# Score products on 64 rows of the array, queries and keys without a copy

## The chip, the cores and the metric

The kernel runs on one core of one Trainium2 chip. A core has a matrix engine (TensorE, PE in the profile), two elementwise engines that matter here (VectorE or DVE, and ScalarE or ACT), GpSimd (POOL), and a queue (SyncE or SP) that issues the DMA transfers. The metric is the device time of one execution in microseconds. The time of the kernel before is 1354.46 us, the median of 3 runs (1352.4 to 1356.58).

## The reference, cut to what matters

Two layers of a diffusion block over 512 latent tokens and 256 context tokens, model width 1024, all in float32. The change concerns the mixer of the first layer, differential attention: 8 heads, and per head two softmax maps of head width 64 that share one value matrix of width 128.

```python
def project(t):
    q, k, v = jnp.split(t @ wqkv, 3, axis=-1)
    return (q.reshape(B, n, DA_HEADS, 2, HEAD_DIM),
            k.reshape(B, n, DA_HEADS, 2, HEAD_DIM),
            v.reshape(B, n, DA_HEADS, DA_VDIM))

def attend(qb, kk, vv):
    s = jnp.einsum('bqhmd,bkhmd->bhmqk', qb, kk) * scale
    p = jax.nn.softmax(s, axis=-1)
    p = p[:, :, 0] - lam_full * p[:, :, 1]
    return jnp.einsum('bhqk,bkhe->bqhe', p, vv)

q, k, v = project(h)                     # 512 latent tokens
q, k = apply_rope_2d(q, cos, sin), apply_rope_2d(k, cos, sin)
qc, kc, vc = project(hc)                 # 256 context tokens
k_all = jnp.concatenate([kc, k], axis=1)
```

After the mixer come its output projection, a SwiGLU feed-forward, a second layer with a gated short convolution and its own feed-forward, and a final norm.

## The kernel before, in words

**Precision.** TensorE reads 32-bit operands in a rounded form (`F32R`). To keep float32 accuracy, each operand is split into a high part (the rounded value) and a low part (the remainder): `split` (lines 54 to 56) rounds on ScalarE and subtracts on VectorE. A product is then hi*hi + hi*lo + lo*hi, three matmuls into one accumulator (`mm3`, lines 77 to 81).

**Layout.** Activations lie transposed: channels on the 128 partitions, tokens along the free dimension. One head's query projection is a tile of 128 partitions by 512 tokens; its first 64 partitions belong to map 0, the other 64 to map 1.

**Queries and keys of a head.** `proj_qk_steps` (line 468) loads and splits the weights, runs the projections (accumulators psq, psk and, for context keys, pskc) and calls `finish_q` and `finish_k`. Both rotate with `rope` (four VectorE instructions) and split into high and low part, in the staging tiles qt (128 x 2 x 512) and kt (128 x 2 x 768), of which there is one buffer each. Then `halves_to` (line 414) copies by DMA, on the SP queue, into one pair of tiles per map: for queries, the map's 64 rows are put twice, into the lower and the upper 64 partitions of qs0 or qs1; for keys, the high part goes to the lower 64 partitions of ks0 or ks1 and the low part to the upper 64. That is four transfers of 256 KB for queries and four of 192 KB for keys per head. With these tiles one matmul over 128 rows computes q_hi*(k_hi + k_lo), a second q_lo*(k_hi + k_lo).

**Scores.** `attend` (line 490) goes through four blocks of 128 queries per head. For each map it runs four matmuls at line 507 (two parts j by two column ranges, 512 and 256 keys) into a score tile S of 128 x 768 in PSUM, takes the row maximum on VectorE (line 511) and the exponential on ScalarE (line 515). There are two S buffers. Then the maps are combined (line 523), transposed on TensorE (pt, line 528), copied, and multiplied by the values (po, line 535).

**What sets the order.** The code runs under a tile scheduler, which decides the order of each engine's instructions at build time. Between one head's score products it places the projections of the next head (psq, psk, pskc), the value projection of the next pair of heads (psv), the modulation sums (ada, pada) and, in the last heads, the output projection (poa). Each engine then runs its list strictly in that order.

Of the kernel before, what the change touches and what calls it, by code (L numbers as in the profile page):

```python
# [11 lines left out]
F32 = mybir.dt.float32  # L12
F32R = mybir.dt.float32r
AF = mybir.ActivationFunctionType
ALU = mybir.AluOpType
# [3 lines left out]
P = 128  # L19
# [6 lines left out]
def block_kernel(  # L26
# [11 lines left out]
    nc = tc.nc  # L38
    T = x.shape[1]
# [4 lines left out]
    KV = T + C  # L44
    KB = KV // P
    NH = D // P
    HD = 64
# [6 lines left out]
    def split(hi, lo, src):  # L54
        nc.scalar.copy(hi, src)  # L55
        nc.vector.tensor_tensor(lo, src, hi.bitcast(F32), op=ALU.subtract)  # L56
# [55 lines left out]
    psB = tc.alloc_tile_pool(name="psB", bufs=2, space=PSUM)  # L112
# [8 lines left out]

    for tag, n, bufs in (
        [(f"Or{h}", 512, 1) for h in range(NH)] + [("qs0", 1024, 2), ("qs1", 1024, 2)]
        + [("e", 768, 3), ("pth", 768, 3), ("ptl", 768, 3), ("ks0", 768, 2), ("ks1", 768, 2)]
        + [(f"v{p}{t}", 256, 2) for t in range(KB) for p in "hl"]
        + [("sq", 512, 1), ("dg1", 512, 1)]
        + [(t, 4, 2) for t in ("sv", "sr", "rh", "rl")] + [(t, 4, 3) for t in ("rr", "mx")] + [("ss", 8, 2), ("den", 8, 2)]
        + [("ld", 2, 1)]
        + [("araw", 1024, 2), ("ada", 1024, 1), ("qt", 1024, 1), ("kt", 1536, 1), ("rcos", 512, 1), ("rsin", 512, 1)]
        + [("sw", 512, 1), ("rt", 512, 2)]  # L130
    ):
        ap.tile([P, n], F32, tag=tag, bufs=bufs, name=f"place_{tag}")
# [4 lines left out]
    xt_dram = nc.dram_tensor("xt_spill", [DB, P, T], F32, kind="Internal").ap()  # L137

    rows = lambda v: v.rearrange("(j p) -> j p", p=P)
    st1, st2 = (ap.tile([P, P], F32, tag=t, name=n) for t, n in (("ks1", "st1"), ("ks1", "st2")))  # L140
    nc.vector.memset(st1, 0.0)
    nc.vector.memset(st2, 0.0)
    nc.sync.dma_start(st1[0:8, :], rows(c[0]))
# [26 lines left out]
    cn = [nat(ctx, t, "qs1", 2, f"cn{t}") for t in range(CB)]  # L170
# [28 lines left out]
    def nat_rstd(src, tag, name):  # L199

        nb = len(src)
        ss = ap.tile([P, 8], F32, tag="ss", name=f"ss{name}")
        for t in range(nb):
            for f in range(2):
                junk = ap.tile([P, 512], F32, tag="sq", bufs=1, name=f"junk{name}")
                nc.scalar.activation(
                    junk, src[t][:, f * 512:(f + 1) * 512], AF.Square,
                    accum_out=ss[:, t + 4 * f:t + 4 * f + 1],
                )
        v = ap.tile([P, 4], F32, tag="sv", name=f"sv{name}")[:, :nb]  # L210
        nc.vector.tensor_tensor(v, ss[:, :nb], ss[:, 4:4 + nb], op=ALU.add)
        nc.vector.tensor_scalar(v, v, 1.0 / D, EPS, op0=ALU.mult, op1=ALU.add)
        r = ap.tile([P, 4], F32, tag="sr", name=f"sr{name}")[:, :nb]
        nc.gpsimd.tensor_tensor(r, v, mhalf[:, :nb], op=ALU.pow)
        ps = spread(r, nb, "pt", name)
        o = ap.tile([P, 512], F32, tag=tag, bufs=2 if tag == "ks0" else 1, name=f"rs{name}")[:, :nb * P]
        nc.vector.tensor_copy(o, ps)
        return o

# [40 lines left out]
    for k in range(0, DB, 2):  # L260
        pt = psB.tile([P, 2, T], F32, tag="S", name=f"ptx{k}")
        for a in range(2):
# [2 lines left out]
            nc.vector.tensor_copy(XT0[k + a], pt[:, a, :])  # L265
        if k == 0:
            ada0(0, raws0)
    rc = nat_rstd(cn, "ks0", "c")
    ctt = [ap.tile([P, 4, C], F32, tag="araw", name=f"ct{i}") for i in range(2)]
    CT = [ctt[k // 4][:, k % 4, :] for k in range(DB)]  # L270
    for i in range(2):
        pt = psB.tile([P, 4, C], F32, tag="S", name=f"ptc{i}")
        for a in range(4):
            k = 4 * i + a
# [126 lines left out]
    On = [None] * NH  # L401
    later = []

    def rope(ps, tmp, name):

        r = ap.tile([P, T], F32, tag="rt", name=f"rt{name}")
        b = ap.tile([P, T], F32, tag="sw", bufs=1, name=f"sw{name}")
        nc.vector.tensor_tensor(b, ps, rsin, op=ALU.mult)
        nc.vector.tensor_tensor(r, ps, rcos, op=ALU.mult)
        nc.vector.stream_shuffle(tmp, b, SWAP)  # L410
        nc.vector.tensor_tensor(r, r, tmp, op=ALU.add)
        return r

    def halves_to(dst, src, both):

        for m in range(2):
            s = src[64 * m:64 * m + 64]
            for d in range(2):
                o = dst[m][64 * d:64 * d + 64]
                nc.sync.dma_start(o.bitcast(F32), s if both else s[:, d, :])  # L420

    def finish_q(h, ps):

        qt = ap.tile([P, 2, T], F32, tag="qt", bufs=1, name=f"qt{h}")
        r = rope(ps, qt[:, 1, :], f"q{h}")
        nc.scalar.activation(qt[:, 0, :].bitcast(F32R), r, AF.Copy, scale=HD ** -0.5)
        nc.vector.scalar_tensor_tensor(
            qt[:, 1, :].bitcast(F32R), r, HD ** -0.5, qt[:, 0, :], op0=ALU.mult, op1=ALU.subtract
        )
        q = [ap.tile([P, 2, T], F32R, tag=f"qs{m}", name=f"qs{h}_{m}") for m in range(2)]  # L430
        halves_to(q, qt, True)
        return q

    def finish_k(h, ps, psc):

        kt = ap.tile([P, 2, KV], F32, tag="kt", bufs=1, name=f"kt{h}")
        r = rope(ps, kt[:, 1, :T], f"k{h}")
        split(kt[:, 0, T:].bitcast(F32R), kt[:, 1, T:].bitcast(F32R), psc)
        split(kt[:, 0, :T].bitcast(F32R), kt[:, 1, :T].bitcast(F32R), r)
        ks = [ap.tile([P, KV], F32R, tag=f"ks{m}", name=f"ks{h}_{m}") for m in range(2)]  # L440
        halves_to(ks, kt, False)
        return ks

    def finish_v(g, t, ps):
# [45 lines left out]
    def attend(h, between, after=None):  # L490
        q, ks, vs = Q[h], K[h], V[h // 2]
# [3 lines left out]
        for pr in range(2):  # L495
# [3 lines left out]
            for s in range(2):  # L499
                qb = 2 * pr + s  # L500
                e = []
                mx = ap.tile([P, 2], F32, tag="mx", bufs=3, name=f"mx{h}_{qb}")
                for m in range(2):
                    S = psB.tile([P, 1024], F32, tag="S", name=f"S{h}_{qb}_{m}")
                    for a, b in ((0, 512), (512, KV)):
                        for j in range(2):
                            nc.tensor.matmul(  # L507
                                S[:, a:b], q[m][:, j, qb * P:(qb + 1) * P], ks[m][:, a:b],
                                start=(j == 0), stop=(j == 1),
                            )  # L510
                    nc.vector.tensor_reduce(  # L511
                        out=mx[:, m:m + 1], in_=S[:, :KV], axis=AX.X, op=ALU.max, negate=True
                    )
                    em = ap.tile([P, KV], F32, tag="e", bufs=3, name=f"e{h}_{qb}_{m}")
                    nc.scalar.activation(  # L515
                        em, S[:, :KV], AF.Exp, bias=mx[:, m:m + 1], accum_out=den[:, m, qb:qb + 1]
                    )
                    e.append(em)
# [5 lines left out]
                for kh in range(2):  # L524
                    pt = psB.tile([P, 512], F32, tag="pt", name=f"pt{h}_{qb}_{kh}")[:, :3 * P]
                    for i in range(3):
                        k = 3 * kh + i
# [410 lines left out]
```

## Time and profile before

| | |
|---|---|
| median of 3 runs | 1354.46 us (1352.4 to 1356.58) |
| profiled execution, its own time | 1355.16 us |
| its span | 1353.4 us |
| mean granted TensorE clock | 0.993 of full speed |
| TensorE busy | 1309.2 us (97%) |
| VectorE busy | 749.5 us (55%) |
| ScalarE busy | 502.6 us (37%) |
| score products (line 507) | 256 matmuls, from 107.1 to 388.5 us |
| copies of q and k (line 420) | 64 transfers, 14 MB of 182.78 MB |

Busy time counts each instruction from its start to its modelled end; matmuls overlap, so the steps between their starts tell what each one takes of the engine. PEld is the load of the stationary operand, which TensorE normally does during the matmul before. In rows of the timeline the columns are start, length, engine, line, operation, output<-inputs, shape, count, and in brackets the idle time before and what ended it. Neighbouring instructions of one line may be merged into one row with their count.

### The profile page before, as it was taken

To read this page: it belongs to the slowest core of one execution; us is meant where nothing else is said; L and a number is where in the kernel's file an instruction comes from. 1 tells how busy PE (TensorE), PEld (TensorE's weight loads), DVE (VectorE), ACT (ScalarE), POOL (GpSimd) and SP (SyncE) were. 2 spreads that over 40 slices of the span, in tenths; PEclk is the share of its full clock that TensorE was granted. 3 is DMA by queue.
4 is the path that set the end of the run, shared out by engine and by line. 5 is a ranking of instruction groups with operands and counts; after the bars stand their busy time and mean duration, and the time that the engine had idled before them with its cause. 6 is when DMAs were issued, how large, how long until landed. Compare 5 with 4: busy or idle time off the path is not lost.

```text
span 1353.4 us, 17631 instructions
## 1 busy us (share of the span) xinstructions
PE 1309.2 (97%) x6972; PEld 1122.9 (83%) x6972; DVE 749.5 (55%) x1001; ACT 502.6 (37%) x841; POOL 98.1 (7%) x103
## 2 busy tenths in 40 slices
PE   6789999999999999999999999999999999999997
PEld 4668889998889888888788899888898888888887
DVE  6787865856767776676742264444463333332222
ACT  7534543554555433232232253222452222322122
POOL 2100000000014000000000050000430000000000
PEclk9999999999999999999999999999999999999999
DMA  9866634623632676767633323333233333333321
GB/s 300 257 208 167 198 78 154 163 71 94 172 122 66 187 218 215 220 218 217 210 102 92 95 79 109 94 94 101 83 97 93 94 102 101 94 90 113 100 72 63
DMA packets 238741, 182.78 MB, mean 135 GB/s; under 512 B 6937, under 2 KB 220226, under 8 KB 238658
## 3 DMA queue, kind: packets, MB, share of 16 engines
q1 hardware_dynamic: 238658, 181.65, 45.3%
q8 instruction: 55, 0.90, 0.3%
q14 instruction: 28, 0.23, 0.1%
HBM read 162.75 MB, written 4.19 MB: 123 GB/s over the span
## 4 chain that ended last, share of the span: by engine, by line
PE 83%; DVE 6%; DMA 5%; ACT 3%; issue 1%; POOL 1%; SPq 0%; ACTq 0%; DVEq 0%; POOLq 0%
PE po_fo L79 6%; PE po_fo L80 6%; PE po_fo L81 6%; PE pb L80 6%; PE pb L81 6%; PE pb L79 6%; PE pa L79 5%; PE pa L80 5%; PE pa L81 5%; DMA araw<-in_ada_w_dram 3%; PE S L507 3%; PE po L535 3%; PE pt L528 1%; DVE ada L365 1%; PE psv L80 1%
## 5 line engine op out<-in xcount | busy, mean ns | idle before, releaser
L55 ACT CAST whi_f<-raw_f 128x1024 fp32r<-128x1024 f32 x87 | 91.4, 1051 | 233.1 <-issue 119.1
L56 DVE TENSOR_TENSOR wlo_f<-raw_f,whi_f 128x1024 fp32r<-128x1024 f32 x87 | 107.4, 1235 | 78.8 <-ACT whi_f L55 75.9
L56 DVE TENSOR_TENSOR wlo_fo<-raw_fo,whi_fo 128x1024 fp32r<-128x1024 f32 (+1 forms) x48 | 54.5, 1136 | 118.4 <-ACT whi_fo L55 117.1
L79 PE MATMUL po_fo<-uh,whi_fo 128*128 128x512 f32 (+1 forms) x324 | 118.7, 366 | 0.1
L80 PE MATMUL po_fo<-ul,whi_fo 128*128 128x512 f32 (+1 forms) x324 | 118.6, 366 | 0.0
L81 PE MATMUL po_fo<-uh,wlo_fo 128*128 128x512 f32 (+1 forms) x324 | 118.4, 365 | 0.0
L365 DVE SCALAR_TENSOR_TENSOR ada<-araw,sil,ada 128x1024 f32<-128x1024 f32 x70 | 89.8, 1282 | 47.0 <-DMA araw<-in_ada_w_dram 46.8
L55 ACT CAST whi_fo<-raw_fo 128x1024 fp32r<-128x1024 f32 (+1 forms) x48 | 47.1, 981 | 177.6 <-PE po_fo L80 146.9
L515 ACT ACTIVATE e<-S,mx 128x768 f32<-128x768 f32 x64 | 57.8, 905 | 55.6 <-DVE mx L511 54.0
L780 DVE TENSOR_TENSOR uu<-sl,pb 128x512 f32<-128x512 f32 (+1 forms) x48 | 30.8, 641 | 81.6 <-PE pb L81 77.3
L511 DVE TENSOR_REDUCE mx<-S 128x1 f32<-128x768 f32 x64 | 60.3, 951 | 21.6 <-PE S L507 21.4
L81 PE MATMUL pb<-h2h,wlo_f 128*128 128x512 f32 (+1 forms) x192 | 71.8, 374 | 0.0
L79 PE MATMUL pa<-h3h,whi_f 128*128 128x512 f32 (+1 forms) x192 | 71.5, 373 | 0.0
L80 PE MATMUL pb<-h2l,whi_f 128*128 128x512 f32 (+1 forms) x192 | 71.3, 372 | 0.0
L79 PE MATMUL pb<-h2h,whi_f 128*128 128x512 f32 (+1 forms) x192 | 71.3, 372 | 0.0
L81 PE MATMUL pb<-h3h,wlo_f 128*128 128x512 f32 (+1 forms) x192 | 71.3, 371 | 0.0
L79 PE MATMUL pb<-h3h,whi_f 128*128 128x512 f32 (+1 forms) x192 | 71.3, 371 | 0.0
L81 PE MATMUL pa<-h3h,wlo_f 128*128 128x512 f32 (+1 forms) x192 | 71.3, 371 | 0.0
L80 PE MATMUL pb<-h3l,whi_f 128*128 128x512 f32 (+1 forms) x192 | 71.3, 371 | 0.0
L80 PE MATMUL pa<-h3l,whi_f 128*128 128x512 f32 (+1 forms) x192 | 71.1, 371 | 0.0
L79 PEld LDWEIGHTS po_fo<-uh,whi_fo 128*128 128x128 f32 x324 | 61.1, 189 | 10.3 <-DVE on L867 0.3
L80 PEld LDWEIGHTS po_fo<-ul,whi_fo 128*128 128x128 f32 x324 | 61.1, 189 | 9.9
(330 smaller groups left out, 3367.0 us busy)
## 6 DMA issues: line engine op xcount, KB each, us to landing
raw_f<-in_ffn_w_in_dram SPq DMA_DIRECT2D x88, 512.0 KB, 3.7
araw<-in_ada_w_dram SPq DMA_DIRECT2D x80, 512.0 KB, 4.4
raw_fo<-in_ffn_w_out_dram SPq DMA_DIRECT2D x32, 512.0 KB, 3.6
raw_a<-in_ada_w_dram SPq DMA_DIRECT2D x32, 256.0 KB, 4.7
qs<-qt SPq DMA_DIRECT2D x32, 256.0 KB, 4.7
raw_wv<-in_da_wqkv_dram SPq DMA_DIRECT2D x12, 512.0 KB, 4.0
ks<-kt SPq DMA_DIRECT2D x32, 192.0 KB, 4.3
raw_fo<-in_ffn_w_out_dram SPq DMA_DIRECT2D x16, 384.0 KB, 3.2
```

The lines of the kernel that those rows point to most:

```text
L55: nc.scalar.copy(hi, src)
L56: nc.vector.tensor_tensor(lo, src, hi.bitcast(F32), op=ALU.subtract)
L79: nc.tensor.matmul(ps, sh, mh, start=start, stop=False)
L80: nc.tensor.matmul(ps, sh, ml, start=False, stop=False)
L81: nc.tensor.matmul(ps, sl, mh, start=False, stop=stop)
L365: nc.vector.scalar_tensor_tensor(acc, raw, s, acc, op0=ALU.mult, op1=ALU.add)
L507: nc.tensor.matmul(S[:, a:b], q[m][:, j, qb * P:(qb + 1) * P], ks[m][:, a:b], start=(j == 0), stop=(j == 1),)
L511: nc.vector.tensor_reduce(out=mx[:, m:m + 1], in_=S[:, :KV], axis=AX.X, op=ALU.max, negate=True)
L515: nc.scalar.activation(em, S[:, :KV], AF.Exp, bias=mx[:, m:m + 1], accum_out=den[:, m, qb:qb + 1])
L528: nc.tensor.transpose(pt[:, i * P:(i + 1) * P], e[0][:, k * P:(k + 1) * P], ident)
L535: nc.tensor.matmul(po, vs[k][:, vc], pts[k // 3][:, k % 3, :], start=(k == 0), stop=(k == KB - 1))
L780: nc.vector.tensor_tensor(u, s, pb, op=ALU.mult)
```

## The change

The staging tiles and the copies go. `finish_q` and `finish_k` write the split straight into the tiles that the score products read: q (128 x 2 x 512, high and low part, two buffers) and ks (128 x 2 x 768, two buffers, tag kk). The scratch tile of the rotation becomes a tile of its own (tag qt), shared by q and k. The score products read 64 partitions each: map 0 the rows 0 to 63, map 1 the rows 64 to 127, which selects the lower or upper half of the array's rows. Each map now needs three matmuls per column range (hi*hi, hi*lo, lo*hi) in place of two, and the two maps alternate in the written order, which the scheduler has to keep for TensorE (`manual_schedule`).

```diff
-        + [("e", 768, 3), ("pth", 768, 3), ("ptl", 768, 3), ("ks0", 768, 2), ("ks1", 768, 2)]
+        + [("e", 768, 3), ("pth", 768, 3), ("ptl", 768, 3), ("kk", 1536, 2)]
...
-    def rope(ps, tmp, name):
-
+    def rope(ps, name):
+
+        tmp = ap.tile([P, T], F32, tag="qt", bufs=1, name=f"tmp{name}")
         r = ap.tile([P, T], F32, tag="rt", name=f"rt{name}")
...
-    def halves_to(dst, src, both):
-
-        for m in range(2):
-            s = src[64 * m:64 * m + 64]
-            for d in range(2):
-                o = dst[m][64 * d:64 * d + 64]
-                nc.sync.dma_start(o.bitcast(F32), s if both else s[:, d, :])
-
     def finish_q(h, ps):
 
-        qt = ap.tile([P, 2, T], F32, tag="qt", bufs=1, name=f"qt{h}")
-        r = rope(ps, qt[:, 1, :], f"q{h}")
-        nc.scalar.activation(qt[:, 0, :].bitcast(F32R), r, AF.Copy, scale=HD ** -0.5)
+        q = ap.tile([P, 2, T], F32R, tag="qs0", bufs=2, name=f"q{h}")
+        r = rope(ps, f"q{h}")
+        nc.scalar.activation(q[:, 0, :], r, AF.Copy, scale=HD ** -0.5)
         nc.vector.scalar_tensor_tensor(
-            qt[:, 1, :].bitcast(F32R), r, HD ** -0.5, qt[:, 0, :], op0=ALU.mult, op1=ALU.subtract
-        )
-        q = [ap.tile([P, 2, T], F32R, tag=f"qs{m}", name=f"qs{h}_{m}") for m in range(2)]
-        halves_to(q, qt, True)
+            q[:, 1, :], r, HD ** -0.5, q[:, 0, :].bitcast(F32), op0=ALU.mult, op1=ALU.subtract
+        )
         return q
 
     def finish_k(h, ps, psc):
 
-        kt = ap.tile([P, 2, KV], F32, tag="kt", bufs=1, name=f"kt{h}")
-        r = rope(ps, kt[:, 1, :T], f"k{h}")
-        split(kt[:, 0, T:].bitcast(F32R), kt[:, 1, T:].bitcast(F32R), psc)
-        split(kt[:, 0, :T].bitcast(F32R), kt[:, 1, :T].bitcast(F32R), r)
-        ks = [ap.tile([P, KV], F32R, tag=f"ks{m}", name=f"ks{h}_{m}") for m in range(2)]
-        halves_to(ks, kt, False)
+        ks = ap.tile([P, 2, KV], F32R, tag="kk", bufs=2, name=f"ks{h}")
+        r = rope(ps, f"k{h}")
+        split(ks[:, 0, T:], ks[:, 1, T:], psc)
+        split(ks[:, 0, :T], ks[:, 1, :T], r)
         return ks
...
-                for m in range(2):
-                    S = psB.tile([P, 1024], F32, tag="S", name=f"S{h}_{qb}_{m}")
+
+                Ss = [psB.tile([P, 1024], F32, tag="S", name=f"S{h}_{qb}_{m}") for m in range(2)]
+                with tc.manual_schedule(engines={mybir.EngineType.PE}):
                     for a, b in ((0, 512), (512, KV)):
-                        for j in range(2):
-                            nc.tensor.matmul(
-                                S[:, a:b], q[m][:, j, qb * P:(qb + 1) * P], ks[m][:, a:b],
-                                start=(j == 0), stop=(j == 1),
-                            )
+                        for j, (jq, jk) in enumerate(((0, 0), (0, 1), (1, 0))):
+                            for m in range(2):
+                                r = slice(64 * m, 64 * m + 64)
+                                nc.tensor.matmul(
+                                    Ss[m][:, a:b], q[r, jq, qb * P:(qb + 1) * P], ks[r, jk, a:b],
+                                    start=(j == 0), stop=(j == 2),
+                                )
+                for m, S in enumerate(Ss):
                     nc.vector.tensor_reduce(
```

The scheduler's order moves with it. On TensorE, at the first block of head 0, the kernel before has all context-key matmuls (pskc) and then the eight score matmuls, which wait for the copies (DMAHW) and for ScalarE. In names as S_0_1 the first number is the block and the second the map.

```order
L80 MATMUL pskc_1297<-cl_166,whi_wk_1228 128x256
L81 MATMUL pskc_1297<-ch_165,wlo_wk_1229 128x256
L507 MATMUL S_0_0_1066<-ks_0_1055,qs_0_1038 128x512 [waits DMAHW5_49,DMAHW3_49,DMAHW6_49,DMAHW1_49,Activation_49]
L507 MATMUL S_0_0_1066<-ks_0_1055,qs_0_1038 128x512
L507 MATMUL S_0_0_1066<-ks_0_1055,qs_0_1038 128x256 x2
L507 MATMUL S_0_1_1074<-ks_1_1056,qs_1_1039 128x512 [waits DMAHW4_49,DMAHW2_49,DMAHW7_49,DMAHW0_49,Activation_49]
L507 MATMUL S_0_1_1074<-ks_1_1056,qs_1_1039 128x512
L507 MATMUL S_0_1_1074<-ks_1_1056,qs_1_1039 128x256 x2
L79 MATMUL psv_0_1351<-whi_wv_0_1341,hh_135 128x256 [waits DVE_49]
```

In the changed kernel, at the same place, the first pair stands ahead of the context-key matmuls and the other ten products among them.

```order
L81 MATMUL psk_1284<-hh_148,wlo_wk_1246 128x512
L499 MATMUL S_0_0_1055<-ks_1038,q_1028 128x512 [waits Activation_49]
L499 MATMUL S_0_1_1056<-ks_1038,q_1028 128x512
L79 MATMUL pskc_1309<-ch_150,whi_wk_1245 128x256 [waits DVE_49]
...
L80 MATMUL pskc_1309<-cl_161,whi_wk_1245 128x256
L499 MATMUL S_0_0_1055<-ks_1038,q_1028 128x512 [waits DVE_49]
L499 MATMUL S_0_1_1056<-ks_1038,q_1028 128x512
...
L499 MATMUL S_0_1_1056<-ks_1038,q_1028 128x256
L81 MATMUL pskc_1309<-ch_160,wlo_wk_1246 128x256
```

The first pair no longer waits for a transfer, and the block is cut into two runs of score products, with 17 context-key matmuls between.

At the third block of head 0 (S_2) the changed kernel's TensorE list has one product of map 0 alone, seven value-projection matmuls, and then the other eleven, which start with map 1.

```order
L79 MATMUL psv_2_1412<-whi_wv_0_1348,hh_138 128x256
L499 MATMUL S_2_0_1148<-ks_1038,q_1028 128x512 [waits Activation_49]
L80 MATMUL psv_2_1412<-wlo_wv_0_1349,hh_138 128x256
...
L80 MATMUL psv_2_1412<-wlo_wv_1_1355,hh_142 128x256
L499 MATMUL S_2_1_1149<-ks_1038,q_1028 128x512 [waits Activation_49]
L499 MATMUL S_2_0_1148<-ks_1038,q_1028 128x512
L499 MATMUL S_2_1_1149<-ks_1038,q_1028 128x512
L499 MATMUL S_2_0_1148<-ks_1038,q_1028 128x512
```

Here the lone product waits for its own buffer's exponential on ScalarE, and map 1's for the other's.

On the SP queue the kernel before issues, behind the modulation weights (araw), the copies of two heads, with value weights (raw_wv) between them:

```order
L360 DMA araw_3_1_1912<-in_ada_w_dram 128x1024
L420 DMA qs_0_1038<-qt_1029 64x1024 x2
L420 DMA qs_1_1039<-qt_1029 64x1024 x2
L420 DMA ks_0_1055<-kt_1044 64x768
L420 DMA ks_1_1056<-kt_1044 64x768
...
L70 DMA raw_wv_0_1764<-in_da_wqkv_dram 128x4x256
```

The changed kernel goes from the modulation weights straight to the weights of the next head:

```order
L360 DMA araw_3_1_1951<-in_ada_w_dram 128x1024
L70 DMA raw_wv_0_1789<-in_da_wqkv_dram 128x4x256
L70 DMA raw_wv_1_1795<-in_da_wqkv_dram 128x4x256
L70 DMA raw_wq_2060<-in_da_wqkv_dram 128x8x128
L70 DMA raw_wk_2066<-in_da_wqkv_dram 128x8x128
```

The lists of VectorE and ScalarE have as many rows as before; the order of some of them moves.

## Rows read from the trace of the kernel before

**Rows 1.** The page's first part: busy us, share of span, instructions.
```profile
PE 1309.2 (97%) x6972; PEld 1122.9 (83%) x6972; DVE 749.5 (55%) x1001; ACT 502.6 (37%) x841; POOL 98.1 (7%) x103
```

**Rows 2.** Windows: stretch and length, busy PE, PEld, DVE, ACT, POOL, clock, DMA, GB/s.
```profile
95.00:130.00 35.00, 32.20 (x215) 29.76 (x214) 24.69 (x39) 15.63 (x30) 0.00 (x0) 0.95 0.64 161
130.00:165.00 35.00, 34.29 (x206) 30.10 (x205) 30.78 (x48) 17.36 (x35) 1.92 (x1) 1.00 0.71 208
...
235.00:270.00 35.00, 35.00 (x222) 31.66 (x221) 30.39 (x48) 18.20 (x36) 1.01 (x1) 1.00 0.63 170
```

**Rows 3.** Line 507's matmuls: count, least, median, greatest ns, first and last start.
```profile
L507 PE MATMUL S<-ks,qs x256: 274/389/765, 107.1 to 388.5; 128*128 128x512 f32 x64, 128*128 128x256 f32 x64
```

**Rows 4.** Timeline of PE, one map's four score products and the next matmul.
```profile
112.85 0.86 PE L507 MATMUL S<-ks,qs 128*128 128x512 f32 x4
113.55 0.28 PE L79 MATMUL psv<-whi_wv,hh 128*128 128x256 f32 x1
```

**Rows 5.** Timeline of PE, first score products of head 0 and of head 2.
```profile
107.07 2.90 PE L507 MATMUL S<-ks,qs 128*128 128x512 f32 x8 [2.80 <-ACT qt L426]
109.76 0.41 PE L79 MATMUL psv<-whi_wv,hh 128*128 128x256 f32 x1
...
170.26 0.81 PE L507 MATMUL S<-ks,qs 128*128 128x512 f32 x3 [2.74 <-issue]
...
175.35 0.40 PE L79 MATMUL psq<-hh,whi_wq 128*128 128x512 f32 x1
```

**Rows 6.** Windows behind the two idle times.
```profile
107.00:110.00 3.00, 2.93 (x10) 2.58 (x11) 2.18 (x5) 1.04 (x3) 0.00 (x0) 0.50 0.09 30
...
170.20:175.00 4.80, 4.74 (x20) 3.94 (x20) 2.96 (x3) 1.47 (x3) 0.00 (x0) 0.66 0.04 12
```

**Rows 7.** Timeline of SP's queue, the k copies of heads 0 and 2.
```profile
99.47 3.79 SPq L420 DMA_DIRECT2D ks<-kt  x4
...
161.74 1.10 SPq L420 DMA_DIRECT2D ks<-kt  x2
```

**Rows 8.** Timeline of DVE, the wait for q's staging tile.
```profile
104.32 0.01 DVE L410 LOAD_MASK_SELECT qt<-swq  x1 [4.65 <-DMA qs<-qt]
```

**Rows 9.** Timeline of PE and PEld around 4-row products.
```profile
66.36 0.39 PE L80 MATMUL kps<-hl,w0h 128*128 128x512 f32 x1
...
66.59 0.40 PE L81 MATMUL kps<-hh,w0l 128*128 128x512 f32 x1
...
66.92 0.20 PEld L248 LDWEIGHTS pmt<-ident,mr 4*128 4x128 f32 x2 [0.36 <-issue]
...
67.13 0.28 PE L240 MATMUL pm<-whi_a,cst 128*4 128x256 f32 x1
```

**Rows 10.** Timeline of PE, a restart behind an idle time.
```profile
74.08 0.39 PE L81 MATMUL vps<-w0h,cl 128*128 128x256 f32 x1 [0.38 <-DVE cl L224]
74.30 0.28 PE L79 MATMUL vps<-w0h,ch 128*128 128x256 f32 x1
```

**Rows 11.** Timeline of PE, one-column products, transposes, and the next matmul.
```profile
304.87 0.95 PE L552 MATMUL pq<-ones_f,sq 128*128 128x1 f32 x8
305.68 0.52 PE L528 MATMUL pt<-ident,e 128*128 128x128 f32 x3
305.96 0.47 PE L79 MATMUL psk<-hh,whi_wk 128*128 128x512 f32 x1
```

**Rows 12.** Timeline of PE, a change from 128 to 4 columns.
```profile
60.68 0.28 PE L81 MATMUL vps<-ch,w0l 128*128 128x256 f32 x1
60.80 0.28 PE L240 MATMUL pm<-wlo_a,cst 128*4 128x256 f32 x1
```

**Rows 13.** Groups of instructions, the maximum and the exponential.
```profile
L511 DVE TENSOR_REDUCE mx<-S 128x1 f32<-128x768 f32 x64 | 60.3, 951 | 21.6 <-PE S L507 21.4
L515 ACT ACTIVATE e<-S,mx 128x768 f32<-128x768 f32 x64 | 57.8, 905 | 55.6 <-DVE mx L511 54.0 <-DVE e L523 0.8 <-DVE rr L521 0.5
```

More of the change, by code (lines that the diff above doesn't have):

```diff
@@ L139, in block_kernel @@
     rows = lambda v: v.rearrange("(j p) -> j p", p=P)
-    st1, st2 = (ap.tile([P, P], F32, tag=t, name=n) for t, n in (("ks1", "st1"), ("ks1", "st2")))
+    st1, st2 = (ap.tile([P, P], F32, tag=t, name=n) for t, n in (("kk", "st1"), ("kk", "st2")))
     nc.vector.memset(st1, 0.0)
@@ L215, in nat_rstd @@
         ps = spread(r, nb, "pt", name)
-        o = ap.tile([P, 512], F32, tag=tag, bufs=2 if tag == "ks0" else 1, name=f"rs{name}")[:, :nb * P]
+        o = ap.tile([P, 512], F32, tag=tag, bufs=1, name=f"rs{name}")[:, :nb * P]
         nc.vector.tensor_copy(o, ps)
@@ L267, in block_kernel @@
             ada0(0, raws0)
-    rc = nat_rstd(cn, "ks0", "c")
+    rc = nat_rstd(cn, "kt", "c")
     ctt = [ap.tile([P, 4, C], F32, tag="araw", name=f"ct{i}") for i in range(2)]
```

## The prediction

> **What bounds the kernel now.** I read the page's totals first, then a table of stretches for the attention part, then the TensorE timeline inside it. TensorE is busy 97% of the span [rows 1]. The score products run from 107.1 to 388.5 us [rows 3], that is 32 blocks (8 heads of four 128-query blocks) in 281 us, 8.8 us a block. The reader is to see PE at 35.00 of 35.00 us in the stretch from 235, with DVE at 30, and below that in the earlier ones, from 95 and 130 [rows 2]. So TensorE's issue sets the end here, and a microsecond put into or taken out of its queue between 200 and 390 us moves the end by about as much. DVE is the next bound: 30.78 of 35 in the stretch from 130.
>
> The recorded length of a matmul overlaps the next one, so I use steps from start to start. Four score matmuls (two of 512, two of 256 columns) take 113.55 - 112.85 = 0.70 us [rows 4], a 256-column one 60.80 - 60.68 = 0.12 [rows 12], a 512-column one 66.59 - 66.36 = 0.23 [rows 9]; 2 x 0.23 + 2 x 0.12 = 0.70 fits.
>
> **The change, part by part.**
>
> *Score matmuls.* Before: 4 per map, two maps, 32 blocks: 64 x 0.70 = 44.8 us of TensorE time. After: 12 of 64 rows per block, 384 instead of 256. If the two halves of the array work at once, a pair costs what one costs: 3 x (0.23 + 0.12) = 1.05 us a block, 33.6 in all. But the order does not keep all pairs together: the second block of head 0 shows a lone 512-column product of map 0, projection work, then eleven others that begin with map 1. I counted 64 runs of score products in the order of TensorE, 22 of them one such lone product. Adding for each run the longer of its two maps at 0.23 and 0.12 gives 38.7 us. So the term is 38.7 - 44.8 = -6.1. No row shows two matmuls at once on half arrays. The bounds: one after the other, 384 at the same mean price, 67.2 us, +22.4; all pairs together, -11.2. I take -6.1 because the two maps use separate rows, separate tiles and separate banks, and the row of nearest shape (below) shows that a smaller row group is a mode of its own.
>
> *Entering and leaving 64-row work.* The trace has one place where the row count changes: the 4-row products that turn the modulation sums, among 128-row matmuls. The 512-column matmul before them starts at 66.59; its successor should start 0.23 later, at 66.82, and starts at 66.92: 0.10 lost, and its weight load, which normally stands one matmul ahead, starts with it [rows 9]. Two of them end at 67.13, 0.21, which is what two loads cost where nothing hides them: eight one-column products take 305.68 - 304.87 = 0.81, 0.10 each [rows 11]. So leaving shows no drain of its own, but the next load is again not ahead. What a load that is not ahead costs stands at 74.08: the next matmul starts 0.22 later instead of 0.12, 0.10 more [rows 10]. One visit to 64-row work then costs 0.10 (drain) + 0.10 (load) going in and 0.10 (load) coming out, 0.30, and 64 visits 19.2 us, in a stretch where TensorE has nothing to hide it under. Bounds: 0, by the change from 128 to 4 columns, which costs nothing (the step from 60.68 to 60.80 is one) [rows 12], and 25.6 with a drain on both sides. I take 19.2, as the row-count case is the nearer row.
>
> The Trainium skill, "TensorEngine Tiling (Array Packing)", Key Properties, says that changing the tiling mode, unlike changing the tile, drains TensorE. The 0.10 at 66.92 agrees; the rule speaks against this change, since a run of the new products stands among 128-row matmuls on both sides. By the rule with a drain each way the term would be the 25.6 above.
>
> *The copies.* The 64 copies through SP (four each of q and k per head) go, and with them two stands of TensorE. At head 0 the last k copy is issued by 99.47 + 3.79 = 103.26 [rows 7]; TensorE stands idle 2.80 before it starts the scores at 107.07, and then runs slowly: eight matmuls take 109.76 - 107.07 = 2.69 instead of 1.40 [rows 5]. The granted clock is 0.50 there, the lower of its two levels (1.2 GHz), after that idle time [rows 6]. Together 2.80 + 1.29 = 4.1. At head 2 TensorE stands 2.74 before 170.26, and from there to 175.35 takes 5.09 for eight score products, six transposes and six 512-column products [rows 5], at a granted clock of 0.66 [rows 6]. At full clock these are 1.40 + 2 x 0.28 (three transposes, 305.96 - 305.68 [rows 11]) + 6 x 0.23 = 3.34: 2.74 + 1.75 = 4.5. The k copy of that head was issued by 161.74 + 1.10 = 162.84 [rows 7], so I give this stand to the copy, though the profile names no releaser. The sum is -8.6. Bounds: 0, if another wait stands there, and -8.6. DVE also stood 4.65 before it could reuse q's staging tile [rows 8]; that goes too, which makes it likely that the work behind arrives in time. I take -8.6. What is late next at head 0 is nothing that I see: its first pair waits for ScalarE alone (k's high half), and the order has context-key matmuls behind it.
>
> *What costs nothing.* DVE and ScalarE run as many instructions as before (983 and 743 rows in both orders), writing the final tiles directly. The rotation's scratch tile is now shared by q and k; DVE runs both in turn anyway. SP loses 64 issues; the weight loads behind them then start earlier, but they wait for buffers that the DVE split frees, so I count nothing. The products of a block now need both score buffers empty: both maxima (0.95 each), the second exponential (0.90) and 1.2 of products make 4.0 us [rows 13], inside the 8.8 us of a block, and the order puts projection work between. If that cover fails, TensorE stands behind the first product of map 1, and everything behind waits with it.
>
> *Sum.* The profiled execution took 1355.16 us (span 1353.4), 0.7 above the median of 1354.46. 1355.16 - 6.1 - 8.6 + 19.2 = 1359.7, against the median 1359.0: **1359 us**, 0.3% slower.
>
> **Rivals.**
>
> *No price for changing the row count.* For it: a change of columns is free [rows 12], and the loss at 66.92 is one sample of transposes of a 32-row kind. Against: its load is plainly not ahead. Time: 1359 - 19.2 = 1340, faster. The sign turns where a visit costs (6.1 + 8.6) / 64 = 0.23 us.
>
> *Loads of the two halves take turns.* Each product still brings a 128-column load; if the loads share one path at 0.10 [rows 11], a pair of 256 columns is bound by 0.21, not 0.12. Starting each product of a run no earlier than one load behind the one before, the runs come to 45.9 us: the gain of 6.1 becomes a loss of 1.1, and the time 1359 + 7.2 = 1366. For it: 0.10 for one-column products shows a load-bound step. Against: nothing shows loads into separate rows. The Trainium skill, "TensorE: Matmul & The Clock Gate", LDWEIGHTS, says that a load's time goes by its columns and that a load of 32 rows takes as long as one of 128; the 0.10 agrees for 128 rows, and no run here shows 64.
>
> *The halves do not work at once.* Then the products cost 67.2: 1359 + 28.5 = 1388. Against: separate rows and banks. For: no row shows it.
>
> *Another wait replaces the copies'.* TensorE stands at the same places for DVE (30.78 of 35 from 130) or for both score buffers: 1359 + 8.6 = 1368.
>
> **How the numbers follow.** A measurement here can tell about 0.3%, 4 us, from no change. Chances: my forecast 0.36 (own range 1352 to 1366), free switching 0.26, loads in turn 0.18, halves in turn 0.10, replaced wait 0.10. Below 1350.4: nearly all of free switching and 0.03 of the forecast, 0.27. Within 4 us: 0.15 of the forecast and the edges of the others, 0.20. Above 1358.5: the rest, 0.53. The range goes from a little under free switching, 1338, to beyond loads in turn and the replaced wait, 1374; halves in turn stay out.
>
> **What would show it.** In the timeline after, two score products of different maps should start within a few hundredths of each other, a 512-column pair every 0.23; if they start 0.1 apart, loads take turns, at 0.23 each the halves do. The step from the last 128-row matmul to the first score product should be its own plus 0.10, and the first matmul behind a run should again have its load beside it. The idle times before 107 and 170 should be gone, with a full clock in both stretches. Wrong would be: visits without that loss (then 1340), or idle time of TensorE before score products that waits for an exponential.

## The result, and the profile after

The changed kernel takes 1369.38 us, the median of 5 runs (1363.7 to 1371.18), against 1354.46 in the same job: ratio 1.0109, interval [1.0093, 1.0126], which is 14.8 us more (12.6 to 17.1). It is slower, as forecast, and by three times as much as the 4.5 us that the forecast gave. The profiled execution is the shortest one, 1363.7 us with a span of 1361.9.

The page's first part, which answers to [rows 1]: TensorE is busy 14.6 us longer, with 128 more matmuls.

```profile
PE 1323.8 (97%) x7100; PEld 1116.7 (82%) x7100; DVE 751.9 (55%) x1001; ACT 500.9 (37%) x841; POOL 96.8 (7%) x103
```

Windows of the changed kernel, columns as in [rows 2]:

```profile
95.00:130.00 35.00, 35.00 (x243) 30.34 (x242) 24.87 (x41) 16.31 (x34) 0.00 (x0) 1.00 0.17 49
130.00:165.00 35.00, 35.00 (x212) 28.82 (x211) 29.12 (x42) 15.09 (x29) 1.45 (x1) 1.00 0.62 190
165.00:200.00 35.00, 35.00 (x235) 29.43 (x231) 21.51 (x37) 16.41 (x35) 1.01 (x1) 1.00 0.11 33
...
270.00:305.00 35.00, 35.00 (x226) 30.14 (x225) 17.22 (x29) 14.19 (x30) 0.00 (x0) 0.95 0.15 46
```

PE is now busy 35.00 of 35.00 in every stretch from 95 to 340, at full clock up to 270: the stands of [rows 5] are gone. (From 340 to 375 it is 33.50, behind waits for VectorE and ScalarE ahead of the output projection.) So up to there the loss is work on TensorE, no wait.

The score products as a group, which answers to [rows 3] (count, least, median and greatest ns, first and last start). They start 8 us earlier and end 12.5 us later.

```profile
L499 PE MATMUL S<-ks,q x384: 271/384/502, 98.9 to 401.0; 64*128 64x512 f32 x101, 64*128 64x256 f32 x91
```

The timeline of TensorE at the first block of head 0 and at the third, which answers to [rows 4]. The x2 row is a pair of one product of each map, the x1 row a lone product; the x11 row is the rest of the lone one's block.

```profile
98.92 0.50 PE L499 MATMUL S<-ks,q 64*128 64x512 f32 x2
99.35 0.38 PE L79 MATMUL pskc<-ch,whi_wk 128*128 128x256 f32 x1
...
112.38 0.28 PE L79 MATMUL psv<-whi_wv,hh 128*128 128x256 f32 x1
112.59 0.49 PE L499 MATMUL S<-ks,q 64*128 64x512 f32 x1
113.01 0.39 PE L80 MATMUL psv<-wlo_wv,hh 128*128 128x256 f32 x1
113.23 0.28 PE L81 MATMUL psv<-whi_wv,hl 128*128 128x256 f32 x1
113.35 0.28 PE L79 MATMUL psv<-whi_wv,hh 128*128 128x256 f32 x1
...
113.82 0.28 PE L80 MATMUL psv<-wlo_wv,hh 128*128 128x256 f32 x1
114.03 1.31 PE L499 MATMUL S<-ks,q 64*128 64x512 f32 x11
115.28 0.39 PE L81 MATMUL psv<-whi_wv,hl 128*128 128x256 f32 x1
115.50 0.28 PE L79 MATMUL psv<-whi_wv,hh 128*128 128x256 f32 x1
```

Two things are read here. First, the pair takes 99.35 - 98.92 = 0.43, the lone product 113.01 - 112.59 = 0.42: two products on the two halves cost what one costs, loads included. Second, the price of a visit stands around the lone product. The 256-column matmul ahead takes 112.59 - 112.38 = 0.21 instead of 0.12 (0.09 more), the product 0.42 instead of 0.23 (0.19 more), the matmul behind 113.23 - 113.01 = 0.22 instead of 0.12 (0.10 more), and the next again 0.12: 0.38 in all. That the loads are no longer ahead stands in the rows of PEld, where each of the two starts with its own matmul:

```profile
112.59 0.18 PEld L499 LDWEIGHTS S<-ks,q 64*128 64x128 f32 x1
113.01 0.19 PEld L80 LDWEIGHTS psv<-wlo_wv,hh 128*128 128x128 f32 x1 [0.24 <-issue]
```

The rest, 0.09 on either side, I call the drain; no row shows it as an instruction of its own. The run of eleven has the same: 1.25 for products of 1.05, 0.09 ahead, 0.10 behind. The Trainium skill, "TensorEngine Tiling (Array Packing)", Key Properties, says that a change of mode drains the engine and that different tiles load and multiply in parallel; these rows agree with both.

To compare kernels I add this up over all runs of score products in the timeline: from a run's start to the next matmul behind it, plus what the matmul ahead and the one behind take beyond their usual steps (0.12 for 256 columns, 0.23 for 512), waits included. I call it the score sum.

| kernel | runs of score products | score sum, us | against before: ratio, interval |
|---|---|---|---|
| before | 61 | 54.3 | 1 |
| changed | 64 | 64.8 | 1.0109 [1.0093, 1.0126] |
| maps in turn | 68 | 88.0 | 1.0278 [1.0258, 1.0298] |
| changed, with copies | 68 | 66.4 | 1.0127 [1.0108, 1.0146] |
| before, without copies | 61 | 45.6 | 0.9962 [0.9948, 0.9976] |
| 45 runs | 45 | 54.6 | 1.0019 [1.0006, 1.0031] |
| 39 runs | 39 | 51.4 | 1.0015 [1.0005, 1.0026] |
| 32 whole runs | 32 | 49.5 | 1.0006 [0.9996, 1.0016] |

### The profile page after: what moved, and what is told of

It reads as the page before. It is cut to its first block, busy times and chain, and to the rows that moved or that the text cites. A ratio compares the mean times of both kernels' runs of the same rounds, so it can differ in the third digit from the quotient of the medians.

```text
span 1361.9 us, 17727 instructions
## 1 busy us (share of the span) xinstructions
PE 1323.8 (97%) x7100; PEld 1116.7 (82%) x7100; DVE 751.9 (55%) x1001; ACT 500.9 (37%) x841; POOL 96.8 (7%) x103
## 4 chain that ended last, share of the span: by engine, by line
PE 88%; DVE 4%; DMA 4%; ACT 1%; issue 1%; SPq 1%; POOL 0%; DVEq 0%; ACTq 0%; POOLq 0%
PE po_fo L79 6%; PE po_fo L80 6%; PE po_fo L81 6%; PE pa L79 6%; PE pb L80 5%; PE pa L80 5%; PE pb L81 5%; PE pb L79 5%; PE pa L81 5%; PE S L499 4%; PE po L528 3%; DMA araw<-in_ada_w_dram 2%; PE pt L521 2%; PE psv L80 1%; PE psv L81 1%; PE psv L79 1%
## 5 line engine op out<-in xcount | busy, mean ns | idle before, releaser
L79 PEld LDWEIGHTS po_fo<-uh,whi_fo 128*128 128x128 f32 x324 | 61.1, 189 | 10.3 <-DVE on L860 0.3
L81 PEld LDWEIGHTS po_fo<-uh,wlo_fo 128*128 128x128 f32 x324 | 61.1, 189 | 9.9
```

The lines of the kernel that those rows point to most:

```text
L79: nc.tensor.matmul(ps, sh, mh, start=start, stop=False)
L81: nc.tensor.matmul(ps, sl, mh, start=False, stop=stop)
```

## The experiments

Differences are of ratios to the kernel before that ran beside each kernel, times 1354 us, unless medians are named.

**The changed kernel again.**

> The changed kernel once more, for a second profile, since the one at hand is its shortest execution (1363.7 us, mean granted clock 0.996) and the four others took 1368.8 to 1371.2 at 0.990 to 0.995. Theory that the extra 5 us are TensorE at its lower clock for longer: a profile near 1369 shows one or two more stretches of 35 us with a granted clock under 1.00, and the same number of steps in the score products at full clock. Rival, that the score products themselves sometimes run slower: then a block's steps at clock 1.00 are longer than in the first profile (twelve products 1.24 us to the next instruction, a lone one 0.42).

It took 1368.47 us (span 1366.7). The score sum is 64.8 again, so the products did not run slower. From 95 on to the end of the scores, either profile has one stretch with a granted clock under 1.00: the first the one from 270 (above), the second this one (windows, columns as above):

```profile
340.00:375.00 35.00, 33.50 (x180) 25.72 (x179) 23.02 (x40) 16.63 (x35) 1.01 (x1) 0.95 0.25 80
```

These two offset each other. The stretch that only the second profile has at less than full clock lies ahead of them, first profile first:

```profile
60.00:95.00 35.00, 28.49 (x171) 22.80 (x170) 31.04 (x50) 14.04 (x26) 2.85 (x2) 1.00 0.74 227
60.00:95.00 35.00, 28.38 (x167) 22.82 (x166) 30.15 (x48) 13.74 (x25) 2.86 (x2) 0.95 0.75 228
```

The two run the same list, so they can be laid beside each other matmul by matmul. The second is 2.1 us later at the first query projection of head 1 (89.86 against 87.77, behind VectorE in both), 3.4 after the fall of the clock that follows there, 2.3 after the fall that only the first has (at 294), 3.6 after the second's own (at 363), and 4.8 at the end. So the theory holds for a part: one more fall of the clock, 1.3 us, of 4.8. The median of the five, 1369, is the usual time, and the first profile is a short one.

**The maps in turn.** Is it the alternation that lets two products run at once?

```diff
-                    for a, b in ((0, 512), (512, KV)):
-                        for j, (jq, jk) in enumerate(((0, 0), (0, 1), (1, 0))):
-                            for m in range(2):
-                                r = slice(64 * m, 64 * m + 64)
+                    for m in range(2):
+                        r = slice(64 * m, 64 * m + 64)
+                        for a, b in ((0, 512), (512, KV)):
+                            for j, (jq, jk) in enumerate(((0, 0), (0, 1), (1, 0))):
```

> The changed kernel with the maps one behind the other: map 0's six 64-row products and then map 1's six, so that no two products on different halves stand beside each other (except at the seam). 68 runs instead of 64. Theory that a pair runs at once: the products go from about 39 us to at most 67.2, so about 22 to 28 us slower than the changed kernel, 1391 to 1397. Rival that the halves gain nothing from alternating: 1.5 us slower, from the four additional runs.

Measured: 1391.5 us, 23 more than the changed kernel, and a score sum 23.2 larger, as the theory has it. Timeline of this kernel, six products of one map:

```profile
116.52 1.32 PE L499 MATMUL S<-ks,q 64*128 64x512 f32 x6
117.76 0.39 PE L81 MATMUL psv<-whi_wv,hl 128*128 128x256 f32 x1
```

Six products of one map take 1.24, as long as eleven or twelve in alternation. The halves work at once when the neighbours in the order lie on different halves.

**The price of a visit, first try.** One product of 4 columns is added behind each map's four, over 64 rows, and as a control over 128.

```diff
+                    nc.tensor.matmul(
+                        S[:, KV:KV + 4], q[m][0:64, 0, qb * P:(qb + 1) * P], ks[m][0:64, 0:4],
+                        start=True, stop=True,
+                    )
```

> The kernel before with one more product behind each map's four score products: 64 rows, 128 columns loaded, 4 columns streamed, into unused columns of the score tile; it adds 64 visits to 64-row work and nothing that is read. Beside it runs the same product over 128 rows, so the difference of the two is the price of the visits alone. My forecast's price of 0.30 us gives 19 us of difference; the price read in the trace after, 0.385 us (a drain and a load that is not ahead, on both sides), gives 25 us; no price for the row count gives 0.

> The control: the kernel before with one more product behind each map's four, over 128 rows, 4 columns streamed, into unused columns of the score tile. Every theory expects only the product itself, at most the step of a one-column product, 0.10 us, so 64 x 0.10 = 6.4 us over the kernel before, at least 64 x 0.002 = nothing that can be measured.

Measured: 1.0183 [1.0163, 1.0203] and 1.0054 [1.0035, 1.0072]; the difference is 17.5 us, 0.27 a visit. That is near my forecast's 0.30, and it misleads. Timeline, 64 rows first:

```profile
114.85 0.86 PE L507 MATMUL S<-ks,qs 128*128 128x512 f32 x4
115.64 0.27 PE L511 MATMUL S<-ks,qs 64*128 64x4 f32 x1
115.84 0.39 PE L79 MATMUL psv<-whi_wv,hh 128*128 128x256 f32 x1
116.06 0.28 PE L80 MATMUL psv<-wlo_wv,hh 128*128 128x256 f32 x1
```

And the control:

```profile
114.88 0.17 PE L511 MATMUL S<-ks,qs 128*128 128x4 f32 x1
114.91 0.36 PE L79 MATMUL psv<-whi_wv,hh 128*128 128x256 f32 x1
115.11 0.28 PE L80 MATMUL psv<-wlo_wv,hh 128*128 128x256 f32 x1
```

The visit itself shows 0.09 ahead (0.79 for products of 0.70), 0.20, and 0.10 more behind: 0.39. But the control's short product leaves the load of the second matmul behind it uncovered, 115.11 - 114.91 = 0.20 instead of 0.12, so the control holds a part of the price. Against the kernel before, the 64-row product costs 0.0183, 24.8 us or 0.39 a visit, as the rows say.

**The price of a visit, second try.** The same with 256 columns, long enough to cover a load.

```diff
-                        S[:, KV:KV + 4], q[m][0:64, 0, qb * P:(qb + 1) * P], ks[m][0:64, 0:4],
+                        S[:, KV:KV + 256], q[m][0:64, 0, qb * P:(qb + 1) * P], ks[m][0:64, 0:256],
```

> The price of a visit once more, now with a product long enough to cover the load behind it: the kernel before with one more 64-row product of 256 columns behind each map's four, into unused columns of the score tile. Its control is the same product over 128 rows. In the first pair the control's 4-column product left the next load uncovered (115.11 - 114.91 = 0.20 for a product of 256 columns), so that the difference of 17 us lacked a part of the price. With drains and uncovered loads on both sides the difference is 64 x 0.385 = 24.6 us; by my forecast's 0.30 it is 19.2; if leaving costs neither drain nor load, 64 x 0.19 = 12.

> The control of the longer visit: the kernel before with one more 128-row product of 256 columns per map. Every theory expects its step, 64 x 0.12 = 7.7 us over the kernel before.

Measured: 1.0230 [1.0201, 1.0259] and 1.0046 [1.0026, 1.0066]. The control alone costs 6.2 us (7.7 were expected). The difference, 0.0184, is 24.9 us, 0.39 a visit (medians 1384.06 and 1360.37: 23.7 us, 0.37). Timeline with 64 rows:

```profile
116.87 0.86 PE L507 MATMUL S<-ks,qs 128*128 128x512 f32 x4
117.66 0.38 PE L511 MATMUL S<-ks,qs 64*128 64x256 f32 x1
117.97 0.38 PE L79 MATMUL psv<-whi_wv,hh 128*128 128x256 f32 x1
118.19 0.28 PE L80 MATMUL psv<-wlo_wv,hh 128*128 128x256 f32 x1
```

And its control:

```profile
114.54 0.86 PE L507 MATMUL S<-ks,qs 128*128 128x512 f32 x4
115.23 0.28 PE L511 MATMUL S<-ks,qs 128*128 128x256 f32 x1
115.35 0.28 PE L79 MATMUL psv<-whi_wv,hh 128*128 128x256 f32 x1
115.47 0.28 PE L80 MATMUL psv<-wlo_wv,hh 128*128 128x256 f32 x1
```

From the four score products to the second matmul behind: 118.19 - 116.87 = 1.32 against 115.47 - 114.54 = 0.93. The 0.39 lie in three steps: 0.79 against 0.69 (drain going in), 0.31 against 0.12 (load that is not ahead, and drain coming out), 0.22 against 0.12 (load coming out). So the whole price is shown by times and rows, and its split into loads and drains by rows alone.

**The copies, put back.** q and k are staged and copied by DMA again, for the 64-row products.

```diff
+    def copy_to(dst, src):
+        for m in range(2):
+            s = slice(64 * m, 64 * m + 64)
+            for d in range(2):
+                nc.sync.dma_start(dst[s, d, :].bitcast(F32), src[s, d, :])
```

> The changed kernel with q and k staged again and copied by DMA before the score products read them (eight transfers a head), score products as in the changed kernel, 68 runs of them. Theory that the copies cost the two stands of TensorE of heads 0 and 2 in the kernel before (4.1 and 4.5 us): this kernel is 8.6 us slower than the changed one, plus 4 x 0.385 = 1.5 for its four additional runs, so about 10 us, and the idle times before the first scores of heads 0 and 2 are back. Rival, that these stands came from the order of the kernel before and not from the copies: 1.5 us slower, with no idle time there.

Measured: 1371.94 us, ratio 1.0127 against 1.0109: 2.4 us more (by the two intervals, good to about 3.4), where the theory says 10 and the four additional runs account for 1.5. No stand came back before the first scores of heads 0 and 2. The one that this kernel has is behind VectorE, at the rotation of head 1's key, which VectorE reached late behind other work (timeline):

```profile
150.05 0.39 PE L79 MATMUL psv<-whi_wv,ch 128*128 128x256 f32 x1 [2.54 <-DVE rtk L409]
```

The rival holds: copies need not cost a stand, if the order has other work there.

**The copies, left out of the kernel before.** q and k are written as in the changed kernel, and the score products keep 128 rows.

```diff
-                                S[:, a:b], q[m][:, j, qb * P:(qb + 1) * P], ks[m][:, a:b],
+                                S[:, a:b], q[:, j, qb * P:(qb + 1) * P], ks[:, m, a:b],
```

> The kernel before without the copies alone: q and k are written once, where the projection leaves them, and the score products keep 128 rows, four per map, as before. Since the two maps are not separated then, the scores are other numbers; the work of every engine but the copies is that of the kernel before. My prediction's term, two stands of TensorE owed to the copies, gives 8.6 us less than before, 1345.7. Rival, for which the staged version of the changed kernel speaks (2.8 us more with copies, 1.5 of them its four additional runs): the stands belong to the order around the copies, and leaving the copies out brings 1 to 3 us, 1352.

Measured: 1347.98 us, 0.9962 [0.9948, 0.9976], 5.1 us less (3.2 to 7.0; by medians 6.6). It lies between theory and rival. The score sum fell by 54.3 - 45.6 = 8.7, as the theory says, and the first scores now stand among context-key work with no idle time (timeline, then windows):

```profile
101.98 0.85 PE L497 MATMUL S<-ks,q 128*128 128x512 f32 x4
102.67 0.28 PE L79 MATMUL pskc<-ch,whi_wk 128*128 128x256 f32 x1
```

```profile
95.00:130.00 35.00, 35.00 (x242) 32.57 (x241) 28.16 (x44) 18.63 (x37) 0.00 (x0) 1.00 0.18 57
165.00:200.00 35.00, 35.00 (x219) 31.55 (x217) 23.14 (x39) 17.66 (x37) 1.01 (x1) 1.00 0.20 61
```

So the stands go with the copies in that order, and are worth 8.7 in these rows, but by the times only 5 to 6.6 of it reach the end. (The profiled execution, the shortest of its five, took 1345.45, 9.7 under the profiled one of the kernel before.) Where the rest goes is open.

**Fewer visits.** If a run costs 0.39, keeping a block's twelve products together must pay. The first product also waits until both score tiles are free; the second kernel adds a high priority for the block.

```diff
+                                if a == j == m == 0 and last_exp:
+                                    tc.add_manual_dep(mm.ins, last_exp[-1].ins.name, ...)
```

> As the kernel with both changes, but without the priority: the first product of a block also waits for the second exponential of the block before; 45 runs of score products instead of 64. Theory of 0.385 us a run: 19 x 0.385 = 7.3 us less plus 2 to 3 for pairing: about 10 us under the changed kernel, 3 us behind the version with 39 runs. Rival with no price for a run: 2 to 3 us less than the changed kernel, and equal to the version with 39 runs. Rival of the added wait: slower than the changed kernel.

> The changed kernel with a block's twelve score products kept together more often: the first one also waits for the second exponential of the block before, and the block has a high priority in the scheduler; 39 runs of score products in the order instead of 64, 28 of them whole blocks. My theory, that each run costs about 0.385 us for going to 64 rows and back (read in the trace after): 25 fewer runs x 0.385 = 9.6 us less, and the lone products paired (38.7 down to about 35) another 3 to 4: 13 less than the changed kernel, about 1355. Rival with no price for a run (only the products themselves cost more than forecast): 3 to 4 us less, about 1365. Rival that the added wait costs more than it saves: TensorE idle before score products with an exponential as its releaser, and no gain.

Measured: 1.0019 and 1.0015, that is 12.2 and 12.7 us less than the changed kernel. Expected were 10 and 13, so a run has its price; with no price the gain would be 2 to 4. That 39 runs bring hardly more than 45 was not expected; of the forecasts, only the rival's without a price has them equal, and its sizes are wrong. Waits take it back: timeline of the kernel with 45 runs,

```profile
154.18 1.31 PE L500 MATMUL S<-ks,q 64*128 64x512 f32 x12 [0.58 <-ACT e L515]
236.48 1.31 PE L500 MATMUL S<-ks,q 64*128 64x512 f32 x12 [1.64 <-ACT e L515]
```

and of the one with 39, where VectorE holds transposes back:

```profile
228.80 0.55 PE L530 MATMUL pt<-ident,e 128*128 128x128 f32 x3 [2.32 <-DVE sv L559]
```

**All blocks whole.** Only the second to twelfth product have the high priority, and a head's first block waits for the low parts.

```diff
+                                hp = nullcontext() if a == j == m == 0 else tc.high_priority()
+                                with hp:
...
+                                if a == j == m == qb == 0:
+                                    for low in (qlow[h], klow[h]):
+                                        tc.add_manual_dep(mm.ins, low.ins.name, ...)
```

> A version that is meant to beat both: all twelve score products of a block stand together in the order of TensorE, 32 runs. The first one waits for the second exponential of the block before and, in a head's first block, for the low parts of q and k; the other eleven have a high priority in the scheduler, the first one has none. By the price of 0.385 us a run read in the trace of the changed kernel: 32 x (1.05 + 0.385) = 45.9 us for the score products against 64.8 in the changed kernel, 19 less: 1350 if TensorE never stands for the added waits. The version with 45 runs stands 0.58 and 1.64 us behind an exponential; if these stay, 1352. Rival that fewer runs bring no more (45 and 39 runs gave the same 1356 to 1357): 1356.

Measured: 1356.0 us (11 runs), 1.0006 [0.9996, 1.0016]: no difference from the kernel before, 14 us under the changed one. The theory's 1350 to 1352 missed; the rival's 1356 came. The score sum is 4.8 lower than before, yet the time is not. Timeline of VectorE and TensorE in this kernel:

```profile
230.59 1.28 DVE L365 SCALAR_TENSOR_TENSOR ada<-araw,sil,ada 128x1024 f32<-128x1024 f32 x1 [0.60 <-DMA araw<-in_ada_w_dram]
231.80 1.01 DVE L535 SCALAR_TENSOR_TENSOR e<-e,rr,e 128x768 f32<-128x768 f32 x1
232.73 1.81 DVE L521 TENSOR_REDUCE mx<-S 128x1 f32<-128x768 f32 x2
```

```profile
232.96 0.85 PE L540 MATMUL pt<-ident,e 128*128 128x128 f32 x6 [1.37 <-DVE e L535]
235.68 1.43 PE L503 MATMUL S<-ks,q 64*128 64x512 f32 x12 [1.88 <-ACT e L525]
```

VectorE does a modulation sum, which itself waits 0.60 for its weights, before it combines the maps and takes the maxima; TensorE stands for both, 1.37 and 1.88.

**VectorE relieved.** The kernel with whole runs, with the mixer's modulation sums cut from 1024 to 64 columns.

```diff
-                nc.vector.scalar_tensor_tensor(acc, raw, s, acc, op0=ALU.mult, op1=ALU.add)
+                w = D if spread_sum else 64
+                nc.vector.scalar_tensor_tensor(acc[:, :w], raw[:, :w], s, acc[:, :w], op0=ALU.mult, op1=ALU.add)
```

> The version with 32 whole runs, with the modulation sums of the first layer's mixer part cut from 1024 to 64 columns (all but the first of each eight), which leaves 15/16 of them out: 21 VectorE instructions of 1.28 us become short ones. Theory that VectorE, late with maximum and combination behind these sums, takes back what the fewer runs gain (TensorE stands 0.75, 1.37 and 1.88 us in that version): the stands go, 4 us less than the version with whole runs, 1352 or below. Rival, that the gain is lost in the price of the runs itself or in clock: no difference.

Measured: 1345.69 us, 0.9946 [0.9928, 0.9964], 8 us under the version with whole runs (8.5 by medians, each against the kernel before that ran beside it), twice what the three stands add up to. The direction is as the theory says: with shorter work on VectorE the score products no longer stand behind an exponential, though one stand of transposes behind VectorE is left (1.49 before 219.56). A part of the size lies ahead of the scores, where the first query projection of head 1 waits 0.27 for VectorE instead of 2.61 (it starts at 86.53, and at 91.04 in the version with whole runs). What the kernel before would gain from the same cut was not measured, so this does not say that the whole runs are worth 8 us.

## Why the prediction was right in sign and short in size

- **What bounds the kernel.** Right between kernels of the changed form: against the changed kernel, maps in turn add 23.2 to the score sum and 23 to the time, and 45 and 39 runs take 10.2 and 13.4 from the sum and 12.2 and 12.7 from the time. Against the kernel before it comes out in part only: leaving out the copies takes 8.7 from the sum and 5.1 from the time, and the whole runs take 4.8 and nothing.
- **Score matmuls, -6.1.** Right. After: the runs take 51.4 from start to next matmul; without the 0.19 that each of the 64 loses at its ends, 39.2 us, against 44.8: -5.6. The 22 lone products of 512 columns were counted rightly (the first of them is in the third block of head 0, not the second). The rivals of loads or halves in turn fall by the pair of 0.43 against the lone one of 0.42. Luck is in the range: 1369 lies outside the 1352 to 1366 that the forecast gave its own mechanism, and nearest to the rivals at 1366 and 1368, neither of which the rows show.
- **Entering and leaving, +19.2.** This is the step that failed: "So leaving shows no drain of its own". It does: 0.31 for a 256-column product between the modes is load plus drain. The price is 0.38 to 0.39 instead of 0.30, and 64 x 0.385 = 24.6 instead of 19.2. I had taken the 0.21 behind two 4-row products [rows 9] for two uncovered loads; a load and a drain fit it as well, and that row cannot tell them apart; nor can it show the load coming out, since the matmul behind them loads 4 columns, not 128. The upper bound of 25.6 was the better value.
- **The copies, -8.6.** The stands are gone in the changed kernel, and the kernel before without copies shows them as 8.7 in its rows, but its time gained only 5.1 (3.2 to 7.0). And the stands belong to the copies in that order of the work: with copies in the changed kernel's order, none came back. So by the times the term was too large by about 3.5.
- **Sum.** 24.6 - 5.6 - 5.1 = 13.9, inside the measured 12.6 to 17.1. Of the 10 us that the forecast lacked, 5.4 are the visits, 3.5 the copies, 0.5 the products; the rest is within the interval. This sum takes the copies by their time; by the score sum it is 24.6 - 5.6 - 8.7 = 10.3, and some 4 us of the measured 14.8 stay open, as below.
- **What costs nothing.** Right: DVE and ACT are busy 751.9 and 500.9 as against [rows 1], and no score product of the changed kernel stands more than about 0.3 for an exponential (the run at 106.47 takes 1.55 to the next matmul instead of 1.25). That cover is thin: the variants that wait for both score tiles at once do stand, up to 1.88.

Open: the 2 to 6 us by which the medians of all these kernels lie above what their score sums say against the kernel before; some of it is waits around 360 us and ahead of the attention part that differ between executions. In the profiles, the part from the first query projection of head 1 to the last value product (psq to po) follows the score sum within 3 us: 307.2 us before, 317.5 and 319.1 in the two profiles of the changed kernel. But what lies ahead of it takes 87.8 to 91.8 us in the profiles of the kernels in the table, and what lies behind 956.7 to 959.6 (before: 88.6 and 957.6), so that single profiles differ there by as much as is to be explained. No run here separates chance from effect.

## What to carry to other kernels

In these runs products on half the rows run two at once, but only as direct neighbours in the order, and each stay there costs a drain and an uncovered load on either side, 0.385 us here: before packing, count the stays, not the products, and keep each one whole. A control for such a price must be long enough to cover the next load itself, or it hides part of the price. When a wait on one buffer becomes a wait on two, look which engine sets them free: in this kernel VectorE took back what fewer stays gave.

## What was not expected of the hardware

The clock fell without idle time. Timeline of the changed kernel, then windows before and after (PE busy, clock as the third value from the end):

```profile
290.85 1.31 PE L499 MATMUL S<-ks,q 64*128 64x512 f32 x12
292.10 1.95 PE L372 MATMUL pada<-ones_f,ada 128*128 128x1 f32 x16
293.91 0.58 PE L79 MATMUL psq<-hh,whi_wq 128*128 128x512 f32 x1
```

```profile
291.00:294.00 3.00, 3.00 (x29) 2.73 (x30) 2.91 (x3) 1.29 (x3) 0.00 (x0) 1.00 0.14 35
295.00:297.00 2.00, 2.00 (x6) 1.54 (x6) 1.09 (x6) 1.32 (x4) 0.00 (x0) 0.50 0.97 280
```

TensorE was busy 3.00 of 3.00, but for 1.8 us of it with sixteen products of one column; then the granted clock is 0.50, the lower level (1.2 GHz). The profile's busy share alone does not tell whether the clock will hold. But the one-column products alone do not make it fall: in the second profile of the same kernel the same run of them stands between the same neighbours, and the clock stayed at 1.00 (timeline, then window).

```profile
295.80 1.95 PE L372 MATMUL pada<-ones_f,ada 128*128 128x1 f32 x16
```

```profile
270.00:305.00 35.00, 35.00 (x244) 31.03 (x242) 18.57 (x32) 15.80 (x31) 0.00 (x0) 1.00 0.16 46
```

What decides between the two is not shown.
